# The low parts of two Down weights in each middle quarter: made by an accumulating transfer instead of VectorE, and used last in what is begun

## The chip, the cores and the metric

The kernel runs on one core of a Trainium2 chip. The core has a matrix engine (TensorE, PE in the profile; its weight loads are PEld), three engines for elementwise work (VectorE or DVE, ScalarE or ACT, GpSimd or POOL), and SyncE (SP), which here only issues transfers. Each engine works through its own list of instructions in order and waits at semaphores for the others. The metric is the device time of one execution in microseconds (us), the median of three runs.

## The reference

Two layers, each on 512 positions of width 1024: a gated feed-forward block (FFN) of inner width 2816, a mixer of three head groups, and a second FFN of the same form. The change lies in the FFNs, of which there are four in all:

```python
def swiglu(x, w1, w3, w2):
    return (jax.nn.silu(x @ w1) * (x @ w3)) @ w2
...
h = x + 0.5 * swiglu(rms_norm(x, ffn1_norm[l]), ffn1_w1[l], ffn1_w3[l], ffn1_w2[l])
```

The product with `w1` and `w3` is called Up here, that with `w2` Down. Everything is float32.

## The kernel before

**Precision by parts.** A float32 operand is kept as a high part, which the matrix engine takes at full speed, and a low part, which is the rest. A product is then three matmuls: high by high, high by low, low by high. `mm3` (lines 179 to 182) issues them. Its second line, 181, multiplies the weight's high part by the activation's low part, and line 182 the weight's low part (`wlo`) by the activation's high part (`ghi`). In the profile these three are the rows of L180, L181 and L182.

**Two ways to make the parts of a weight.** `weights` (line 164) loads a piece of weight from HBM into a tile `raw` and splits it. With V as its third argument, `split` (line 147) has ScalarE copy the high part (L148) and VectorE subtract it from `raw` (L149). With G, `split_by_dma` (line 151) has ScalarE write the high part (L153) and then its input with the sign turned (L154; the copy rounds as the high part does), and a transfer issued by GpSimd (L155) adds the weight from HBM a second time, so that the rest is left in the tile. The second way needs no VectorE, one more ScalarE operation, and one more transfer, which can start only when ScalarE is through.

**Stages of an FFN.** The 22 slices of 128 inner columns stand in four quarters of 6, 6, 6 and 4 (`QUARTERS`). For each quarter the Up products of its slices are made, two slices at a time. The first four slices are plain three-matmul products, the later ones (`up_pair`) go by a scheme with seven half-size products, which loads three more tiles of weights: `raw` and sums of weights, `wsum`, of which one half is again added by a transfer from GpSimd (L372). In the first three quarters the Up products of the next quarter's first pair come ahead of this quarter's Down products (`ahead`). Their matmuls are the rows of L383 and L391.

**Down.** For each of the eight blocks `d` of 128 output columns, `begin(d)` loads a weight of 128 x 768 numbers (384 KB), splits it (always with V before) and multiplies the first four of the quarter's six slices; then the last two follow, and VectorE adds the result to `h` (L611). That is 18 matmuls for each `d`, in one bank of PSUM. There are three banks of the kind `mm`, one of which the Up pair uses too, four pairs of tiles for weights' parts (`whi`, `wlo`), and three for `raw`.

**What sets the order.** The text of the program is not the order of issue. A planner puts each engine's instructions into a list when the kernel is built: it takes what is ready by its own reckoning of times, so that matmuls of a Down weight may stand between those of an Up pair. Some places have orders written by hand (`queued`, `issue_after`); `begin` in the first three quarters has none. The list is fixed at run time.

Of the kernel before, what the change touches and what calls it, by code (L numbers as in the profile page):

```python
# [16 lines left out]
ALL = slice(None)  # L17

P = 128
# [46 lines left out]
def trunk(ctx: ExitStack, tc: tile.TileContext, xT, memT, pos, w1a, w3a, w2a, w1b, w3b, w2b,  # L66
          wconv, wqk, wvm, wmem, wout, gains, small, rows, consts, out):
    nc = tc.nc
    V, G, A, T = nc.vector, nc.gpsimd, nc.scalar, nc.tensor
# [10 lines left out]
    turn, tail, hold, opening = [0], [None], {}, []  # L80
# [10 lines left out]
    def bank(shape, tag):  # L91

        if tag == "mm":
            return ps_mm.tile(shape, F32, tag=tag, name=tag)
        return ps_ax.tile(shape, F32, tag=tag, name=tag, bufs=1 if tag == "cf" else 2)
# [7 lines left out]
    def raw_tile(src, cols):  # L103
        raw = wst.tile([P, UNIT], F32, tag="raw", name="raw", bufs=3)
        raw_tile.at = nc.sync.dma_start(raw[:, 0:cols], src)
        return raw
# [40 lines left out]
    def split(hi, lo, x, on):  # L147
        a = A.activation(hi, x, AF.Copy)  # L148
        return a, on.tensor_tensor(out=lo, in0=x, in1=hi.bitcast(F32), op=ALU.subtract)  # L149

    def split_by_dma(hi, lo, x, src):

        A.activation(hi, x, AF.Copy)  # L153
        A.activation(lo, x, AF.Copy, scale=-1.0)  # L154
        G.dma_start(lo, src, accum_op=ALU.add)  # L155
# [6 lines left out]
    def pair():  # L162
        return (wst.tile([P, UNIT], F32R, tag="whi", name="whi"), wst.tile([P, UNIT], F32R, tag="wlo", name="wlo"))

    def weights(src, cols, on, own=None):
        hi, lo = own or pair()
        if first:
            raw = first.pop(0)
            for c in halves:
                opening.append(split(hi[:, c], lo[:, c], raw[:, c], V)[0])  # L170
            return hi, lo
        raw = raw_tile(src, cols)
        if on is G:
            split_by_dma(hi[:, 0:cols], lo[:, 0:cols], raw[:, 0:cols], src)
        else:
            weights.at = split(hi[:, 0:cols], lo[:, 0:cols], raw[:, 0:cols], on)[1]
        return hi, lo

    def mm3(ps, a, b, first, last, **more):
        T.matmul(ps, a[0], b[0], start=first, stop=False, **more)  # L180
        T.matmul(ps, a[0], b[1], start=False, stop=False, **more)  # L181
        tail[0] = T.matmul(ps, a[1], b[0], start=False, stop=last, **more)  # L182

    def at(p, *idx):
        return tuple(x[idx] for x in p)

    def blk(k, n=P):
        return slice(k * n, (k + 1) * n)
# [323 lines left out]
    def ffn(l, w13, w2, x, sums, factors, last, at_product, aside=None, closing=None):  # L512

        def up(f, i, among=(), spread_at=None):
            ps = bank([P, S], "po" if 2 * f + i in (3, 4) else "mm")
            with ExitStack() as held:
                for o in hold.get(2 * f + i, ()):
                    held.enter_context(tc.issue_after(o.ins))  # L520
                w = weights(w13[i][l, f], 1024, V if f == 0 or f < 3 and l == 0 and w13[0] is w1a else G)
            if not among:
                project(ps, w, x)
                return ps
            for k in range(KD):
                with queued():
                    project(ps, w, x, [k])
                for go in among[2 * k : 2 * k + 2]:
                    go()
                if k == spread_at:  # L530
                    r = sums()
                    with queued():
                        scale.append(factors(r))
            return ps

        def gate(pp, R, u, g, hi, lo):
            V.tensor_tensor(out=u, in0=pp[0], in1=R, op=ALU.mult)
            A.activation(u, u, AF.Silu)
            V.tensor_tensor(out=g, in0=pp[1], in1=R, op=ALU.mult)
            V.tensor_tensor(out=g, in0=g, in1=u, op=ALU.mult)  # L540
            split(hi, lo, g, V)

        g, products = {}, []
        for f in range(0, PLAIN, 2):
            g[f], g[f + 1] = gated()
        if first:

            w = [weights(None, 1024, V) for _ in range(2)]
            products = [bank([P, S], "mm") for _ in range(2)]
            steps = [(i, k, *z) for i in range(2) for k, *z in ((0, 0, 0), (0, 0, 1), (1, 0, 0), (1, 0, 1), (0, 1, 0), (1, 1, 0))]  # L550
            steps += [(i, k, *z) for k in range(2, KD) for i, *z in ((0, 0, 0), (0, 1, 0), (1, 0, 0), (1, 1, 0), (0, 0, 1), (1, 0, 1))]
            for n, (i, k, a, b) in enumerate(steps):
                with queued():
                    tail[0] = T.matmul(products[i], w[i][a][:, blk(k)], x[b][:, k, :], start=n in (0, 6), stop=n > 45)
            for d in range(KD):
                with tc.issue_after(opening[-1].ins):
                    squares.add(h[:, d, :])
        while len(products) < at_product:
            products.append(up(len(products) // 2, len(products) % 2))
        among, sums = sums()  # L560
        scale, own = [], w13[0] is w1a
        products.append(up(at_product // 2, at_product % 2, among, (6 if l else 4) if own else KD - 1))
        gain, R, after = scale[0]
        hold.update({i: [kept.at] for i in ((6,) if l else (4, 5))} if own else {})
        if own and not l:
            hold[3] = [squares.at, squares.sum_at]
        while own and not l and len(products) < 5:
            with queued():
                products.append(up(len(products) // 2, len(products) % 2))
        behind = raw_tile.at if own and not l else None  # L570
        M = Seven(normed(gain, R, weights.at if own and not l else None))
        with queued():
            for f in range(0, PLAIN, 2):
                u, v = (tmp.tile([P, 2, S], F32, tag=t, name=t, bufs=n) for t, n in (("u", 1), ("g", 2)))
                for j in range(2):
                    while len(products) < 2 * (f + j) + 2:
                        products.append(up(len(products) // 2, len(products) % 2))
                    gate(products[2 * (f + j) :], R, u[:, j], v[:, j], *g[f + j])
                if not f:
                    M.first()  # L580
        M.rest()
        hold.clear()
        for q, (f0, nf) in enumerate(QUARTERS):
            ahead = 2 if q + 1 < len(QUARTERS) else 0
            for f in range(f0, f0 + nf + ahead, 2):
                if f not in g:
                    g[f], g[f + 1] = up_pair(l, w13, f, M, f > QUARTERS[1][0], behind if f < QUARTERS[1][0] else None)
                    if f == PLAIN:
                        with tc.issue_after(M.gated.ins):
                            rescale = after()  # L590
            begun = []

            def begin(d):

                w = weights(w2[l, d, :, f0 * P : (f0 + nf) * P], nf * P, V)
                ps = bank([P, S], "mm")
                for j in range(nf - 2):
                    mm3(ps, at(w, ALL, blk(j)), g[f0 + j], j == 0, False)
                begun.append((ps, w))

            for d in range(KD if ahead or not closing else KD - 2):
                while len(begun) < (d + 1 if ahead or d else 3):
                    with nullcontext() if ahead or d else queued():
                        begin(len(begun))
                ps, w = begun[d]
                for j in range(nf - 2, nf):
                    mm3(ps, at(w, ALL, blk(j)), g[f0 + j], False, j == nf - 1)
                if not q and rescale:
                    with tc.issue_after((added if d else M.gated).ins):
                        rescale(d)  # L610
                added = V.scalar_tensor_tensor(out=h[:, d, :], in0=ps, scalar=0.5, in1=h[:, d, :], op0=ALU.mult, op1=ALU.add)  # L611
                if not ahead:
                    last(d)
                if aside and q == 2:
                    aside(d, added)
            if closing and not ahead:
                closing(l, f0, nf, g, [at(p, ALL, slice(0, nf * P)) for p in
                                       (weights(w2[l, d, :, f0 * P : (f0 + nf) * P], nf * P, V) for d in range(KD - 2, KD))])
# [765 lines left out]
```

## Time and profile before

| | us |
|---|---|
| median of three runs | 1751.15 (1750.63 to 1751.29) |
| the profiled execution, its own time | 1751.12 |
| its span, first to last instruction | 1749.3 |
| between span and time | 1.8 |

The profile is one execution. Its page gives the busy time of each engine; other views give waits (which instruction stood idle, and what ended that), a timeline (start, length, engine, line, operation, what it writes and reads, how many in a row), groups of like instructions, and transfers. A matmul's length in a row runs on into the next matmul's, since they are pipelined: for the pace of TensorE take the distance between starts.

### The profile page before, as it was taken

What the parts mean: (1) busy time and instruction counts of PE and PEld (TensorE: products, weight loads), DVE (VectorE), ACT (ScalarE), POOL (GpSimd) and SP (SyncE); (2) the same over time, 40 slices, a digit from 0 to 9 for tenths busy, and PEclk for the clock granted to TensorE, in tenths of its full rate; (3) what the DMA queues carried; (4) which work ended last, traced back from release to release, by engine and by line L of the source; (5) the groups of instructions that cost most, each with busy time, mean ns of one, the idle gap of its engine ahead of it and who ended that gap; (6) DMA issues with size and microseconds to landing.
All of it is one profiled execution on the core that took longest, in us unless ns stands there. A gap on an engine that the chain in (4) does not pass through costs nothing.

```text
span 1749.3 us, 25622 instructions
## 1 busy us (share of the span) xinstructions
PE 1735.9 (99%) x9556; PEld 1499.7 (86%) x9556; DVE 1398.0 (80%) x2330; ACT 904.4 (52%) x1437; POOL 193.9 (11%) x220
## 2 busy tenths in 40 slices
PE   9999999999999999999999999999999999999998
PEld 7988888888888988888889888888888889888886
DVE  7968789889877869686778796968898768696966
ACT  6635354555765535353655353535567655353533
POOL 1000000006121000000010000000251310000000
PEclk9999999999999999999999999999999999999999
DMA  8456565357247546464566474643671666474622
GB/s 276 128 140 178 135 166 147 103 160 169 82 93 184 137 131 175 136 177 137 154 146 169 123 185 118 176 140 106 169 161 49 145 145 181 124 186 127 171 79 85
DMA packets 96332, 253.43 MB, mean 145 GB/s; under 512 B 9808, under 2 KB 16208, under 8 KB 96208
## 3 DMA queue, kind: packets, MB, share of 16 engines
q1 hardware_dynamic: 77200, 190.45, 34.1%
q0 software_dynamic: 19008, 61.35, 20.1%
q8 instruction: 75, 1.23, 0.3%
q14 instruction: 49, 0.40, 0.1%
HBM read 249.67 MB, written 2.10 MB: 144 GB/s over the span
## 4 chain that ended last, share of the span: by engine, by line
PE 96%; DVE 2%; ACT 1%; DMA 1%; issue 0%; SPq 0%; DVEq 0%; ACTq 0%
PE po L391 15%; PE mm L180 14%; PE mm L182 14%; PE mm L181 14%; PE pt L391 9%; PE pt L383 8%; PE mm L391 2%; PE cf L391 2%; PE po L383 2%; PE po L180 2%; PE po L182 2%; PE po L181 2%; PE po L989 2%; PE mm L937 1%; PE cf L180 1%; PE cf L182 1%
## 5 line engine op out<-in xcount | busy, mean ns | idle before, releaser
L148 ACT ACTIVATE whi<-raw 128x1024 fp32r<-128x1024 f32 (+3 forms) x346 | 326.1, 948 | 434.0 <-PE mm L181 204.0
L149 DVE TENSOR_TENSOR wlo<-raw,whi 128x1024 fp32r<-128x1024 f32 (+3 forms) x346 | 374.3, 1090 | 70.9 <-ACT whi L148 51.6
L180 PE MATMUL mm<-ghi,whi 128*128 128x512 f32 (+1 forms) x752 | 292.1, 390 | 0.7 <-ACT ghi L508 0.4
L181 PE MATMUL mm<-glo,whi 128*128 128x512 f32 (+1 forms) x752 | 292.3, 389 | 0.0
L182 PE MATMUL mm<-ghi,wlo 128*128 128x512 f32 (+1 forms) x734 | 285.2, 389 | 0.0
L611 DVE SCALAR_TENSOR_TENSOR h<-mm,h 128x512 f32<-128x512 f32 x126 | 86.6, 690 | 139.4 <-PE mm L182 139.1
L180 PEld LDWEIGHTS mm<-ghi,whi 128*128 128x128 f32 x752 | 141.1, 188 | 30.6 <-ACT ghi L508 1.3
L181 PEld LDWEIGHTS mm<-glo,whi 128*128 128x128 f32 x752 | 141.2, 188 | 28.0 <-DVE glo L509 0.4
L182 PEld LDWEIGHTS mm<-ghi,wlo 128*128 128x128 f32 x734 | 137.8, 188 | 27.9
L391 PE MATMUL po<-xlo,whi 128*128 128x512 f32 x512 | 139.5, 394 | 0.0
L1119 DVE SCALAR_TENSOR_TENSOR there<-ypad,par,there 128x512 f32<-128x512 f32 x180 | 136.2, 781 | 1.3
L180 PE MATMUL mm<-xhi,whi 128*128 128x512 f32 x256 | 101.8, 398 | 0.0
L391 PEld LDWEIGHTS po<-xlo,whi 128*128 128x128 f32 x512 | 89.4, 188 | 13.3
L181 PE MATMUL mm<-xlo,whi 128*128 128x512 f32 x256 | 99.6, 389 | 0.0
L182 PE MATMUL mm<-xhi,wlo 128*128 128x512 f32 x256 | 99.5, 390 | 0.0
L148 ACT ACTIVATE whi<-wsum 128x1024 fp32r<-128x1024 f32 x72 | 75.7, 1051 | 33.8 <-PE mm L181 30.2
L149 DVE TENSOR_TENSOR wlo<-wsum,whi 128x1024 fp32r<-128x1024 f32 x72 | 87.8, 1219 | 2.7 <-ACT whi L148 2.7
L391 PEld LDWEIGHTS po<-xlo,wlo 128*128 128x128 f32 x512 | 78.2, 188 | 10.8
L391 PE MATMUL po<-xlo,wlo 128*128 128x256 f32 x512 | 81.3, 280 | 0.0
L440 ACT ACTIVATE part<-pt 128x256 f32<-128x256 f32 x112 | 42.0, 375 | 61.0 <-PE pt L391 61.0
L383 PE MATMUL pt<-mh,whi 128*128 128x256 f32 x512 | 71.7, 283 | 0.0
L383 PEld LDWEIGHTS pt<-mh,whi 128*128 128x128 f32 x512 | 66.6, 191 | 1.0
(410 smaller groups left out, 3659.8 us busy)
## 6 DMA issues: line engine op xcount, KB each, us to landing
raw<-in_w2a SPq DMA_DIRECT2D x48, 384.0 KB, 3.7
raw<-in_w2b SPq DMA_DIRECT2D x48, 384.0 KB, 3.8
raw<-in_w1a SPq DMA_DIRECT2D x26, 512.0 KB, 3.5
raw<-in_w3a SPq DMA_DIRECT2D x26, 512.0 KB, 3.7
raw<-in_w1b SPq DMA_DIRECT2D x26, 512.0 KB, 3.5
raw<-in_w3b SPq DMA_DIRECT2D x26, 512.0 KB, 4.0
wsum<-in_w1a SPq DMA_DIRECT2D x18, 512.0 KB, 6.6
wsum<-in_w3a SPq DMA_DIRECT2D x18, 512.0 KB, 3.8
```

The source lines that it names most:

```text
L148: a = A.activation(hi, x, AF.Copy)
L149: return a, on.tensor_tensor(out=lo, in0=x, in1=hi.bitcast(F32), op=ALU.subtract)
L180: T.matmul(ps, a[0], b[0], start=first, stop=False, **more)
L181: T.matmul(ps, a[0], b[1], start=False, stop=False, **more)
L182: tail[0] = T.matmul(ps, a[1], b[0], start=False, stop=last, **more)
L383: tail[0] = T.matmul(ps, w[part][:, blk(4 * half + q[0])], M.m[j][q[0]][:, q[1]], skip_group_check=True, start=first and not n, stop=n == 11)
L391: tail[0] = T.matmul(out, w[part][:, blk(4 * half + k)], M.m[j][k][:, 0:n], skip_group_check=True, start=first and not part and k == 0, st ...
L440: A.activation(part[i][:, t], x[i][:, 0], AF.Copy)
L611: added = V.scalar_tensor_tensor(out=h[:, d, :], in0=ps, scalar=0.5, in1=h[:, d, :], op0=ALU.mult, op1=ALU.add)
L937: tail[0] = T.matmul(pp[i][:, z, :], q, k, start=not masked, stop=True, skip_group_check=True)
L989: tail[0] = T.matmul(po[:, 2 * c + i, :], ptb[:, i, j, :], v, start=(j == 0), stop=(j == nk - 1))
L1119: V.scalar_tensor_tensor(out=cv[:, c, :], in0=ypad[:, c, j : j + S], scalar=conv_w[:, c, j : j + 1], in1=cv[:, c, :], op0=ALU.mult, op1=AL ...
```

## The change

`begin` takes a new branch for the first two blocks (`d < 2`) of the second and third quarters (`q` is not 0 and `ahead` is not 0), in each of the four FFNs: 2 x 2 x 4 = 16 of the 128 Down weights. There `weights` is called with G, so the low part is made by ScalarE and an accumulating transfer. And the order in which the four slices' matmuls stand in the program is another one: first the high part of the weight by both parts of the activations for all four slices (8 matmuls), then the low part of the weight for all four (4 matmuls). The last two slices are multiplied by `mm3` as before. The number of matmuls is the same.

```diff
             def begin(d):
 
-                w = weights(w2[l, d, :, f0 * P : (f0 + nf) * P], nf * P, V)
+                late = d < 2 and q and ahead
+                w = weights(w2[l, d, :, f0 * P : (f0 + nf) * P], nf * P, G if late else V)
                 ps = bank([P, S], "mm")
                 for j in range(nf - 2):
-                    mm3(ps, at(w, ALL, blk(j)), g[f0 + j], j == 0, False)
+                    if not late:
+                        mm3(ps, at(w, ALL, blk(j)), g[f0 + j], j == 0, False)
+                        continue
+                    for i in range(2):
+                        T.matmul(ps, w[0][:, blk(j)], g[f0 + j][i], start=j == i == 0, stop=False)
+                for j in range(nf - 2 if late else 0):
+                    tail[0] = T.matmul(ps, w[1][:, blk(j)], g[f0 + j][0], start=False, stop=False)
                 begun.append((ps, w))
```

## The prediction

> **What bounds the kernel now.** I read the page first: the busy time of each engine, then the share of each engine in the chain that ended last, then the two kinds of transfer.
>
> ```profile
> span 1749.3 us, 25622 instructions
> PE 1735.9 (99%) x9556; PEld 1499.7 (86%) x9556; DVE 1398.0 (80%) x2330; ACT 904.4 (52%) x1437; POOL 193.9 (11%) x220
> ...
> q1 hardware_dynamic: 77200, 190.45, 34.1%
> q0 software_dynamic: 19008, 61.35, 20.1%
> ...
> PE 96%; DVE 2%; ACT 1%; DMA 1%; issue 0%; SPq 0%; DVEq 0%; ACTq 0%
> ```
>
> TensorE is busy 1735.9 of 1749.3 us and makes 96% of the last chain; VectorE, which the change relieves, makes 2%. But a busy PE could still be waiting inside its pipeline, so next comes the view of waits for PE alone (who waited on whom: us in total, times, longest). It has 11 rows; the first, the two of Down's first matmul, and the last are:
>
> ```profile
> PE mm L554 <- ACT whi L148: 1.2, 1, 1.2
> ...
> PE mm L180 <- ACT ghi L508: 0.4, 2, 0.2
> ...
> PE mm L180 <- ACT whi L148: 0.3, 1, 0.3
> ...
> PE pt L383 <- ACT xlo L148: 0.2, 1, 0.2
> ```
>
> Eleven waits, none over 1.2 us, and no row in which PE waits for VectorE's `wlo` (L149). For Down there is one of 0.3 us. So I look for what the change could break rather than for what it could free, and take one of its eight places apart: the second quarter of the second FFN. The timeline of PE there:
>
> ```profile
> 701.42 0.40 PE L180 MATMUL mm<-ghi,whi 128*128 128x512 f32 x1
> 701.65 0.40 PE L181 MATMUL mm<-glo,whi 128*128 128x512 f32 x1
> 701.88 1.09 PE L391 MATMUL po<-xlo,whi 128*128 128x512 f32 x4
> ...
> 703.27 0.40 PE L180 MATMUL mm<-ghi,whi 128*128 128x512 f32 x1
> ...
> 707.14 0.39 PE L182 MATMUL mm<-ghi,wlo 128*128 128x512 f32 x1
> 707.36 1.07 PE L391 MATMUL pt<-xhi,whi 128*128 128x512 f32 x4
> ...
> 708.74 0.40 PE L182 MATMUL mm<-ghi,wlo 128*128 128x512 f32 x1
> 708.98 1.09 PE L391 MATMUL po<-xlo,whi 128*128 128x512 f32 x4
> ...
> 711.78 0.40 PE L180 MATMUL mm<-ghi,whi 128*128 128x512 f32 x1
> ```
>
> One weight is begun with two matmuls at 701.42, the other does all its 18 from 703.27 to 707.36, and the first goes on at 708.74 and 711.78. Between them stand the last 32 matmuls of the Up pair: 8 at 701.88, 8 at 707.36, 16 at 708.98. From 703.27 to 707.14 there are 17 steps in 3.87 us, 0.228 us each: no gap. Here are the two weights' parts on ScalarE and VectorE, and VectorE's last read of a bank that the 16 matmuls need:
>
> ```profile
> 699.32 0.85 ACT L148 ACTIVATE whi<-raw 128x768 fp32r<-128x768 f32 x1 [1.42 <-issue]
> 700.07 0.36 ACT L440 ACTIVATE part<-pt 128x256 f32<-128x256 f32 x1
> 701.14 0.85 ACT L148 ACTIVATE whi<-raw 128x768 fp32r<-128x768 f32 x1 [0.71 <-PE po L391]
> ...
> 701.37 0.95 DVE L149 TENSOR_TENSOR wlo<-raw,whi 128x768 fp32r<-128x768 f32 x1
> 702.24 0.42 DVE L402 TENSOR_TENSOR part<-part,pt 128x256 f32<-128x256 f32 x1
> 702.57 0.95 DVE L149 TENSOR_TENSOR wlo<-raw,whi 128x768 fp32r<-128x768 f32 x1
> ...
> 704.10 0.42 DVE L402 TENSOR_TENSOR g<-g,po 128x256 f32<-128x256 f32 x1
> ```
>
> I read the other seven places too: the same order, but for one, shown below, that runs 0.5 us behind.
>
> **The change part by part.** Groups of instructions (count, busy us, mean ns), one GpSimd issue, and two rows of transfers (KB each, median us from issue to landing), then the landing of all of L155's:
>
> ```profile
> L149 DVE TENSOR_TENSOR wlo<-raw,whi 128x768 fp32r<-128x768 f32 x96 | 91.6, 955 | 19.1 <-ACT whi L148 18.0
> L154 ACT ACTIVATE glo<-raw 128x768 fp32r<-128x768 f32 x8 | 6.7, 842 | 0.3 <-PE pt L724 0.2
> ...
> 704.83 0.86 POOL L372 DMA_DIRECT2D wsum<-in_w1b  x1 [7.58 <-DVE g L402]
> ...
> glo<-in_wvm POOLq DMA_DIRECT2D x8, 384.0 KB, 8.8
> ...
> DMA to landing us min/median/max: 5.8/8.2/11.8
> ```
>
> Removed: 16 subtractions of 0.955 us, 15.3 us of VectorE. PE does not wait for them anywhere, so they are worth nothing by themselves: 0. What stands behind them on VectorE (the additions of L402) comes up to 1.9 us earlier in each place; that only lets the 24 Up matmuls left after 703.27 go sooner, which is not less work.
>
> Added on ScalarE: 16 copies of 0.842 us, 13.5 us. The second weight's high part, now written from 701.14 to 701.99, comes at most 0.84 us later, 702.83, still ahead of 703.27: 0, with 0.44 us of cover. If that cover is gone, it costs 0.4 us a place at most. `raw` is free after ScalarE's second copy rather than VectorE's subtraction, at 701.3 instead of 702.32, so the next loads from SP start no later.
>
> Added on POOL: 16 issues of 0.86 us, on an engine busy 11%. Ahead of or behind the second one stands L372's issue at 704.83, which waits for its own data; see the rivals.
>
> Added on the DMA engines: 16 transfers of 0.393 MB (384 KB). Queue 0 holds the accumulating ones: 20.1% of 1749.3 us for 61.35 MB is 5.73 us of all sixteen engines per MB, so 2.25 us each, 4.5 a place. That is not free just there. Busy time of the stretches (us, PE, PEld, DVE, ACT, POOL, clock, DMA share, GB/s):
>
> ```profile
> 701.80:707.80 6.00, 6.00 (x30) 5.01 (x29) 3.62 (x9) 1.89 (x5) 0.86 (x1) 1.00 0.97 309
> 707.80:713.80 6.00, 6.00 (x33) 5.15 (x32) 5.86 (x12) 2.92 (x5) 0.00 (x0) 1.00 0.77 194
> 713.80:719.80 6.00, 6.00 (x28) 4.94 (x28) 4.44 (x7) 2.36 (x4) 0.00 (x0) 1.00 0.48 140
> ```
>
> Free are 0.2 us, then 1.4, then 3.1: the backlog is gone by about 719.5 (estimate). It falls on the two low parts, on L372's sums, which are read in the next quarter, or on the Down weights behind, which PE reaches after 712.
>
> Moved: the low part's 4 matmuls go behind 8 others. The wait this brings is the only term that can count. The first low part: high part ready at 700.17, L440 to 700.43, second copy to about 701.3, issue 701.3, landing 8.8 us later (the median for the same size) 710.1; by the ends of L155's row 707.1 to 713.1. The second: 702.8 and 8.8 is 711.6, by the ends 708.6 to 714.6. What PE has without any low part, from 701.42: 2 matmuls (to 701.88), 8 of the Up pair (to 703.27), 8 high ones of the second weight (1.82, to 705.09), 8 of Up (708.74 - 707.36 = 1.38, to 706.47), 16 of Up (711.78 - 708.98 = 2.80, to 709.27; their banks are free at 704.52), 6 high ones of the first weight (1.37, to 710.64). There it needs a low part. If it is the first weight's: there since 710.1, no wait; 4 low matmuls and the last six (2.28) lead to 712.9, and the second's is there since 711.6. No wait again. If it is the second weight's, 711.6 - 710.6 = 1.0 us. A third weight could fill 18 x 0.228 = 4.1 us more, once its bank is free.
>
> The Trainium skill ("DMA: Bandwidth & Descriptors", on the anatomy of one DMA, the GpSimd path) fits 2.0 us and bytes / 436e3 to a transfer from GpSimd. That would be 2.9 us (an estimate by the page): low parts at 704.2 and 705.7, no wait in any order, the same time, and next to no chance for the first rival below. The trace speaks against it, with 5.8 us as the shortest of L155; I go by the row.
>
> Sum: 0 removed, 0 added on engines, wait 0 in eight places: the profiled execution's 1751.12, of which 1749.3 is its span and 1.8 lies around it; the median is 1751.15. I predict **1751.2**.
>
> **The rivals.** *Slower: the low part's matmuls stand in PE's list ahead of its landing.* The list is fixed, so PE then waits with work behind it. Place: the first `wlo` matmul in the eight stages. If the second weight's low part is taken first, 1.0 us x 8 = 8: 1759. If the planner reckons with the shortest landing (708.6 for the second) and the chip needs the median (711.6), 3.0 x 8 = 24: 1775. It decides from 0.44 us a place, 3.5 us in all. For it: the DMA engines at 97% just there. Against it: no row of PE's waits names a transfer, though L155 and L372 are used all through the kernel.
>
> *Slower: the transfers get in each other's way.* It has happened once, in the second quarter of the first FFN:
>
> ```profile
> 175.69 0.86 POOL L372 DMA_DIRECT2D wsum<-in_w3a  x1 [8.79 <-DMA wsum<-in_w3a]
> 176.25 0.33 SPq L105 DMA_DIRECT2D raw<-in_w2a  x1
> ...
> 182.75 0.85 ACT L148 ACTIVATE whi<-raw 128x768 fp32r<-128x768 f32 x1 [2.41 <-DMA raw<-in_w2a]
> ...
> 183.65 0.50 PE L180 MATMUL mm<-ghi,whi 128*128 128x512 f32 x1 [0.31 <-ACT whi L148]
> ```
>
> A load issued behind an accumulating transfer came 6.5 us later, and PE stood 0.31 us. Eight times that is 2.5 us, 1753.6, still within 0.2%. It is more if the second accumulating transfer stands behind L372 on POOL: issue 704.83 + 0.86 = 705.7, landing 714.5 against 712.9, 1.6 us; in the four second quarters, where the timeline has this L372, 6.4 us: 1757.5.
>
> *Faster.* PE's whole waiting in Down is 0.7 us (0.4 and 0.3 above): 1750.4 if all of it went. A better pace from the new order could add to it; but the step is 0.228 from L180 to L181, with the same part of the weight, and from L181 to L182, with another. 0.2% would take 3.5 us, and no row offers that.
>
> *It doesn't do what it says*: the low part made on GpSimd's path but used at once, because the planner mixes the groups. That is the first rival's second price.
>
> **How the numbers follow.** 0.2% (3.5 us) is about what a measurement of this kernel can tell from no change. No wait that counts: 0.56. Low part ahead of its landing: 0.32. Transfers in each other's way by more than 3.5 us: 0.08. Faster: 0.04. So faster 0.04, same 0.56, slower 0.40. The range begins at 1750.3, the faster case, and goes to 1768, a wait of 2.1 us in each place, between the first rival's prices; some 0.15 lie above and 0.03 below. By itself the likeliest case has 1750.6 to 1754.
>
> **What would show it.** VectorE: 80 instead of 96 subtractions of 128x768 on `raw`, about 15 us less busy. ScalarE: 16 rows of L153 and L154 with 128x768 from Down weights. POOL: 16 more issues of L155; queue 0 at 67.6 MB. PE: 9556 matmuls. Right: no row "PE mm <- DMA wlo" of more than a few tenths, and L391's `po` and `pt` matmuls moved ahead of the low parts. Wrong: such a row eight times, with 1 to 3 us each, or PE waiting for `whi` behind late loads. An increase of the time without any new wait of PE would break the whole argument.

## The result, and the profile after

| | before | after |
|---|---|---|
| median, us | 1751.22 (4 runs, 1750.63 to 1751.84) | 1762.28 (4 runs, 1761.94 to 1763.12) |
| ratio, with its 95% interval | | 1.0064 [1.0051, 1.0077] |
| span of the profiled execution, us | 1749.3 | 1760.2 |

The change makes the kernel 11.1 us slower. That lies inside the predicted range (1750.3 to 1768), but the case called likeliest, no wait that counts, did not happen, and the forecast itself, 1751.2, is 11 us too low.

The lines of the page of after that answer to those shown of before: the span, the busy time of each engine, the two kinds of transfer (packets, MB, share of sixteen engines), and the shares of the chain that ended last.

```profile
span 1760.2 us, 25659 instructions
PE 1740.2 (99%) x9556; PEld 1501.4 (85%) x9556; DVE 1384.4 (79%) x2314; ACT 916.1 (52%) x1453; POOL 208.8 (12%) x236
...
q0 software_dynamic: 21312, 67.64, 21.4%
...
PE 90%; DMA 5%; DVE 3%; ACT 1%; issue 1%; POOL 0%; SPq 0%; DVEq 0%; POOLq 0%; ACTq 0%
```

The change did what it says: VectorE has 16 operations fewer and is 13.6 us less busy, ScalarE has 16 more (11.7 us), POOL 16 more, and queue 0 moved 6.29 MB more. PE makes the same 9556 matmuls, but its share of the last chain fell from 96% to 90%, and transfers went from 1% to 5%. Which transfers, the view of PE's waits of after says (us in total, times, longest):

```profile
PE mm L605 <- DMA wlo<-in_w2b: 5.1, 4, 2.1
PE mm L605 <- DMA wlo<-in_w2a: 2.4, 3, 1.4
```

L605 is the new line with the low part's four matmuls. Seven waits, 7.5 us, where before no row named a transfer. That is close to the mark by which the prediction said it would be wrong (such a row eight times, 1 to 3 us each): the seven are 0.4 to 2.1 us long and stand in five of the eight stages. The second quarter of the second FFN, which the prediction took apart, is the worst. Its stage starts at 690.33 us (first Down load issued); here are GpSimd's issues there and ScalarE's copies of the sign-turned high part, from the timeline of after:

```profile
700.85 0.84 ACT L154 ACTIVATE wlo<-raw 128x768 fp32r<-128x768 f32 x1
...
702.68 0.83 ACT L154 ACTIVATE wlo<-raw 128x768 fp32r<-128x768 f32 x1
...
701.98 0.86 POOL L155 DMA_DIRECT2D wlo<-in_w2b  x1 [4.32 <-DVE part L402]
705.92 0.86 POOL L372 DMA_DIRECT2D wsum<-in_w1b  x1 [3.08 <-DMA wsum<-in_w1b]
706.46 1.22 POOL L155 DMA_DIRECT2D wlo<-in_w2b  x1
```

The second low part's transfer could have been issued when ScalarE was through, at 703.5. It was issued at 706.46, behind L372 in POOL's list. L372 adds the second half to a sum of weights (`wsum`) for the next Up pair, and it stood 3.08 us for the load of that sum's first half (L371). That is what the stages have in common: that load lands 13.98 to 15.04 us into the stage, and L372 is issued 0.55 us behind it, in each of the five stages that have such a sum there. In the other three stages POOL's list has no sum between the two low parts.

PE in the same place (timeline of after):

```profile
709.32 0.63 PE L391 MATMUL po<-xlo,wlo 128*128 128x256 f32 x4
710.50 0.50 PE L605 MATMUL mm<-ghi,wlo 128*128 128x512 f32 x1 [0.54 <-DMA wlo<-in_w2b]
...
712.22 0.86 PE L605 MATMUL mm<-ghi,wlo 128*128 128x512 f32 x3
...
714.06 0.39 PE L182 MATMUL mm<-ghi,wlo 128*128 128x512 f32 x1
716.54 1.72 PE L605 MATMUL mm<-ghi,wlo 128*128 128x512 f32 x4 [2.10 <-DMA wlo<-in_w2b]
718.07 0.63 PE L180 MATMUL mm<-ghi,whi 128*128 128x512 f32 x1
718.49 0.63 PE L181 MATMUL mm<-glo,whi 128*128 128x512 f32 x1
...
720.53 0.40 PE L180 MATMUL mm<-ghi,whi 128*128 128x512 f32 x1
```

After 714.06 PE has nothing in its list but the second block's low part, and stands until that lands. Behind the stop its steps are 0.43 us (718.07 to 718.49) instead of 0.23.

Worked out from the timelines of all eight stages, in us from each stage's first Down load (the second low part's issue, its landing, and the start of its four matmuls, which is 23.16 where nothing waits):

| stage | sum between | issued | landed | matmuls |
|---|---|---|---|---|
| 1st FFN, 2nd quarter | yes | 15.36 | 23.94 | 23.98 |
| 2nd FFN, 2nd quarter | yes | 16.13 | 26.17 | 26.21 |
| 2nd FFN, 3rd quarter | yes | 15.62 | 24.77 | 24.82 |
| 3rd FFN, 2nd quarter | yes | 15.93 | 25.31 | 25.36 |
| 4th FFN, 2nd quarter | yes | 15.07 | 24.28 | 24.33 |
| 1st, 3rd, 4th FFN, 3rd quarter | no | 13.47, 14.77, 13.47 | 21.13, 20.99, 20.74 | 23.16 |

The delays of the five add up to 0.82 + 3.05 + 1.66 + 2.20 + 1.17 = 8.9 us (1.25 of it from first low parts that landed late, 0.7 in the second and 0.55 in the third FFN). The slow steps behind the longest stop cost 1.7 us more (716.54 to 720.53 are ten steps, 3.99 us instead of 2.28). Together 10.6, where the spans differ by 10.9.

### The profile page after: what moved, and what is told of

The parts are those of the page before. It is cut to its first block, busy times and chain, and to the rows that moved or that the text cites. A ratio compares the mean times of both kernels' runs of the same rounds, so it can differ in the third digit from the quotient of the medians.

```text
span 1760.2 us, 25659 instructions
## 1 busy us (share of the span) xinstructions
PE 1740.2 (99%) x9556; PEld 1501.4 (85%) x9556; DVE 1384.4 (79%) x2314; ACT 916.1 (52%) x1453; POOL 208.8 (12%) x236
## 4 chain that ended last, share of the span: by engine, by line
PE 90%; DMA 5%; DVE 3%; ACT 1%; issue 1%; POOL 0%; SPq 0%; DVEq 0%; POOLq 0%; ACTq 0%
PE mm L180 13%; PE mm L181 13%; PE mm L182 13%; PE po L391 13%; PE pt L383 8%; PE pt L391 8%; PE cf L391 2%; PE po L383 2%; PE mm L391 2%; PE po L180 2%; DMA wlo<-in_w2b 2%; PE po L182 2%; PE po L181 2%; PE po L996 2%; PE mm L944 1%; DMA wsum<-in_w1a 1%
## 5 line engine op out<-in xcount | busy, mean ns | idle before, releaser
L148 ACT ACTIVATE whi<-raw 128x1024 fp32r<-128x1024 f32 (+3 forms) x330 | 312.6, 952 | 436.0 <-PE mm L181 192.3
L149 DVE TENSOR_TENSOR wlo<-raw,whi 128x1024 fp32r<-128x1024 f32 (+3 forms) x330 | 358.8, 1095 | 87.4 <-ACT whi L148 68.8
L180 PE MATMUL mm<-ghi,whi 128*128 128x512 f32 (+1 forms) x688 | 267.5, 391 | 0.4 <-ACT ghi L508 0.4
L181 PE MATMUL mm<-glo,whi 128*128 128x512 f32 (+1 forms) x688 | 267.7, 389 | 0.0
L182 PE MATMUL mm<-ghi,wlo 128*128 128x512 f32 x670 | 260.5, 389 | 0.0
L180 PEld LDWEIGHTS mm<-ghi,whi 128*128 128x128 f32 x688 | 129.5, 188 | 28.6 <-ACT ghi L508 1.3
L181 PEld LDWEIGHTS mm<-glo,whi 128*128 128x128 f32 x688 | 129.5, 188 | 26.4 <-DVE glo L509 0.4
L182 PEld LDWEIGHTS mm<-ghi,wlo 128*128 128x128 f32 x670 | 126.1, 188 | 25.8
L149 DVE TENSOR_TENSOR wlo<-wsum,whi 128x1024 fp32r<-128x1024 f32 x72 | 87.7, 1217 | 2.7 <-ACT whi L148 2.7
```

## The experiments

Three theories stood after the result. **A**: the second low part's issue stands on POOL behind the waiting L372, and PE's fixed list comes to its matmuls before it lands. **B**: sixteen more transfers in a stretch where the DMA engines are full make every landing late, whatever the order of issue. **C**: the new order of matmuls costs by itself, in pace or in banks. Edits are shown against the changed kernel, with what is left out marked by three dots; "before" is always the kernel before, timed beside it.

**The low parts ahead of the sums on POOL.** The sums' accumulating transfers are held until both low parts' transfers have been issued. PE's list in the eight stages is the same. The edit holds more than the one sum between: each second quarter (and the third quarter of the second FFN) has three sums behind the low parts now, the other third quarters two, and of these the changed kernel issued one 3 to 8 us before the stage and one about 6 us into it, ahead of both low parts.

```diff
-        G.dma_start(lo, src, accum_op=ALU.add)
+        split_by_dma.at = G.dma_start(lo, src, accum_op=ALU.add)
...
-            G.dma_start(x, w13[i][l, f + 1], accum_op=ALU.add)
+            with tc.issue_after(down_low[0].ins) if down_low else nullcontext():
+                G.dma_start(x, w13[i][l, f + 1], accum_op=ALU.add)
...
                 w = weights(w2[l, d, :, f0 * P : (f0 + nf) * P], nf * P, G if late else V)
+                if late:
+                    down_low[:] = [split_by_dma.at]
```

> The changed kernel with one edge more: on POOL the accumulating transfer for the next pair's sum (L372 in the changed kernel) is issued behind both low parts. PE's list stays as in the changed kernel. Theory A (the second low part stands in POOL's queue behind a sum whose own load is late): the second low part is issued about 13.5 us after the stage's first Down load instead of 15.1 to 16.1, lands at about 21 as in the three stages without such a sum, and the waits at the low matmuls fall from about 11 us in all to under 1: 1751 to 1752.5. Theory B (the sixteen DMA engines are full there, whatever POOL's order): landing stays at 24 or later and over half of the waits stay: 1757 or more. Theory C (the new order of the matmuls costs by itself): 1760 to 1763.

Measured: 1753.27 us against 1750.82, ratio 1.0012 [1.0003, 1.0022]. Nine of the 11 us are gone; it is 0.8 us above what A gave. In the third FFN's second quarter (stage start 1038.04), GpSimd's timeline of this kernel, whose lines stand one or two lower (L156 is after's L155, L374 its L372):

```profile
1049.69 0.86 POOL L156 DMA_DIRECT2D wlo<-in_w2a  x1 [23.55 <-ACT wlo L155]
1051.51 0.86 POOL L156 DMA_DIRECT2D wlo<-in_w2a  x1 [0.96 <-ACT wlo L155]
1052.05 1.22 POOL L374 DMA_DIRECT2D wsum<-in_w1a  x1
1052.58 1.58 POOL L374 DMA_DIRECT2D wsum<-in_w3a  x1
1053.12 1.93 POOL L374 DMA_DIRECT2D wsum<-in_w1a  x1
```

The second low part is issued 13.5 us into the stage in all eight places, and lands at 20.8 to 22.6; no matmul of the second block waits for it. In the five stages this landing is earlier by more than the issue: the transfer itself took 7.8 to 9.1 us instead of 8.6 to 10.0, and since two more sums were moved behind it, this run alone doesn't part A from B. But the issue is enough by itself: 13.47 and the lengths that the five had in after make landings of 22.1 to 23.5, against a need at 23.16, or 23.9 in the stage that has the 23.5. So A holds for most of the time. What is left at the low parts is the waits on the *first* one, which lands 5.9 to 8.3 us after its issue; they delay three stages of the profiled execution by 2.1 us in all. Of the 1.35 in the worst of them 0.7 is a later issue (12.34 instead of 11.65, behind ScalarE); the rest is the transfer's length, which is B's cause. That execution, the slowest of the ten, is 3.6 us longer than before's; 1.1 of the rest is a wait at 333.37, outside the stages that the change touches (`PE po L393 <- DVE u L404`). The view of PE's waits has the first low part as

```profile
PE mm L609 <- DMA wlo<-in_w2b: 1.3, 2, 1.1
```

**The order alone.** The new order of matmuls, with the low parts from VectorE again.

```diff
-                w = weights(w2[l, d, :, f0 * P : (f0 + nf) * P], nf * P, G if late else V)
+                w = weights(w2[l, d, :, f0 * P : (f0 + nf) * P], nf * P, V)
```

> The new order of the matmuls, but the low parts from VectorE as before, so no added transfer and nothing added on ScalarE. A and B: no wait at the low matmuls, 1750.7 to 1751.5, as before the change. C: most of the 11 us is there, 1757 or more.

Measured: 1751.59 against 1750.82, ratio 1.0003 [0.9994, 1.0013], span 1749.4, and no wait for `wlo` among PE's. That is 0.1 above what was expected. C falls: the order costs nothing that can be measured.

**The transfer alone.** The low parts by transfer, with the matmuls in the old order.

```diff
-                late = d < 2 and q and ahead
-                w = weights(w2[l, d, :, f0 * P : (f0 + nf) * P], nf * P, G if late else V)
+                slow = d < 2 and q and ahead
+                late = False
+                w = weights(w2[l, d, :, f0 * P : (f0 + nf) * P], nf * P, G if slow else V)
```

> The low parts by the accumulating transfer, but the matmuls in the old order (three for each slice). In PE's list the first low matmul then stands 6.5 us behind the first matmul of the stage (2 + 8 Up + 2 + 8 Up + 16 Up), that is at about 18.1 us, where the first low part lands at 17.7 to 20.1. A and B: waits of about 1 us at the first low part in each of eight stages and 1 to 3 us at the second in five: 1764 to 1770. C: below the changed kernel's time, 1751 to 1757.

Measured: 1779.16 against 1750.82, ratio 1.0158 [1.0143, 1.0174], more than was expected. PE's waits in this kernel:

```profile
PE mm L182 <- DMA wlo<-in_w2b: 10.3, 6, 2.4
PE mm L182 <- DMA wlo<-in_w2a: 8.2, 5, 2.5
```

18.5 us in 11 waits. Behind four of them the granted clock fell (see the last section); counted from windows of 1 us, each fall cost 1.6 to 1.7 us, 6.7 in all. Together that is 25 of the 28 us by which the span is longer than before's; no row names the other 3. So the two halves of the change aren't alike: given the transfer, the new order saves 17 us, and without the transfer (the run above) the order wins nothing.

**Other work in front of the second block's low part.** The third block is begun before the second block's four low matmuls, which now follow the third's 12: 12 x 0.228 = 2.7 us of cover. POOL's list is as in after.

```diff
-                for j in range(nf - 2 if late else 0):
-                    tail[0] = T.matmul(ps, w[1][:, blk(j)], g[f0 + j][0], start=False, stop=False)
                 begun.append((ps, w))
+                if not late:
+                    return
+
+                def low():
+                    with queued() if d else nullcontext():
+                        for j in range(nf - 2):
+                            tail[0] = T.matmul(ps, w[1][:, blk(j)], g[f0 + j][0], start=False, stop=False)
+                lows[d] = low
...
-                while len(begun) < (d + 1 if ahead or d else 3):
+                while len(begun) < (d + 1 + (d == 1 and q > 0) if ahead or d else 3):
...
+                if d in lows:
+                    lows[d]()
```

> The changed kernel, but the second block's four low matmuls stand in PE's list behind the 12 matmuls with which the third block begins (2.7 us), so the second low part is needed at about 26 instead of 23 us. POOL's order is that of the changed kernel. A and B alike (a fixed list with the low part ahead of its landing): only the first low part's waits of about 1 us in all and some tenths at the second stay, 1751.5 to 1753.5. If the time goes into anything but that wait (pace, bandwidth): over 1757.

Measured: 1753.06, ratio 1.0014 [1.0005, 1.0024]. In the stages with a sum between the second low part is still issued at 15.2 to 16.2 and lands at 24.3 to 25.7, as in after; but its matmuls stand at 25.88 (26.4 to 26.6 where the first low part was late), and no block waits for it. The landing is as late as before and costs nothing: what counted is where the list has its reader. What is left is again the first low part (three waits, 1.0 us, in the profiled execution).

**Only the first block by transfer.**

```diff
-                late = d < 2 and q and ahead
+                late = d < 1 and q and ahead
```

> The change for block 0 alone, not block 1: one low part a stage by transfer, issued on POOL ahead of the sum. A: its landing at 18 to 20 us is ahead of its use at about 20.8, no waits: 1750.8 to 1751.8. B: half of the load, half of the loss: 1755 to 1757.

Measured: 1752.16 against 1750.79, ratio 1.0007 [0.9999, 1.0016]; no wait of PE for `wlo`. The first low part is issued 11.7 us into the stage (12.3 in one), ahead of the sum, and lands by 19.9; in this kernel's list its four matmuls stand at 20.87. The median is 0.4 us above what A gave and far below B. What the profiled execution lost, it lost elsewhere: its span is 2.4 us longer than before's, and 1.6 of that come from waits at 331 to 334 us, outside the stages that the change touches.

**Only the second block by transfer.** The same line with `d == 1`.

> The change for block 1 alone: as many transfers as with block 0 alone, but in POOL's queue this one stands behind the sum in five of eight stages. It is needed at about 23.1 us. A: issued at 15 to 16 and landing at 22.5 to 24.5, it is late by up to 1.4 us in those five stages and not in the other three: 1751.5 to 1756, slower than with block 0 alone. B: the same time as with block 0 alone.

Measured: 1754.22, ratio 1.0022 [1.0014, 1.0031]. GpSimd's timeline and PE's, in the third FFN's second quarter of this kernel (stage start 1035.68):

```profile
1050.50 0.86 POOL L372 DMA_DIRECT2D wsum<-in_w1a  x1 [7.76 <-DVE g L402]
1051.03 1.22 POOL L155 DMA_DIRECT2D wlo<-in_w2a  x1
```

```profile
1058.56 0.40 PE L182 MATMUL mm<-ghi,wlo 128*128 128x512 f32 x1
1059.41 1.19 PE L605 MATMUL mm<-ghi,wlo 128*128 128x512 f32 x4 [0.45 <-DMA wlo<-in_w2a]
```

The same standing behind L372, in the same five stages, issued at 15.3 to 15.9. But with one low part in the stage instead of two it lands 6.9 to 8.3 us after its issue (after: 8.6 to 10.0), between 22.7 and 23.7, and is needed at 23.1. So in after the late issue makes 1.6 to 2.7 us of the later landing, and the company of the first low part's transfer another 1.0 to 2.8 (one trace of each): A's place, and some of B in its price. The single transfer lands on the edge: the profiled execution has only this one wait at a low part, and its span, 1751.1, is 1.3 us short of what the median stands for (1754.2 less 1.8 around the span), and the eleven runs go from 1752.85 to 1759.33. Which of the five stages loses more in the other executions no trace here shows.

**Only the third quarters.** The condition is `d < 2 and q == 2`: four stages, of which one has the sum between.

> The change in the third quarters alone (four stages of eight). Only in one of these four does a sum stand between the two low parts on POOL. A: the loss is that one stage's, about 1.8 us: 1752.5 to 1753.5. B: half of the loss, 1756 to 1757.5.

Measured: 1755.46, ratio 1.0026 [1.0015, 1.0037]; 2 us above what A alone gave. The profiled execution's span is 1753.7, and its waits

```profile
PE mm L605 <- DMA wlo<-in_w2b: 2.0, 3, 1.4
...
PE po L391 <- DVE u L402: 0.7, 1, 0.7
```

The 1.4 is the second low part in the one stage with a sum, so that stage pays as in after. Worked out from the timeline, it lost 2.2 us, and another stage lost 0.5 at a first low part: 2.7 of the 4.4 us by which the span is longer than before's. The second row stands at 332.75, outside the changed stages, and the kernel with the order alone, which has no added transfer, has it too (0.3 us, at 332.06); about 0.6 us were lost by there. The rest, about 1 us, stays open. A by itself is too low here, and the measured time is nearer to B's 1756.

**Both remedies.** The low parts ahead of the sums on POOL, and the third block in front of the second's low part.

> Both cures: low parts ahead of the sums on POOL, and the second low part's matmuls behind the third block's beginning. A: no wait at a low part at all, 1750.5 to 1751.5, the same as before the change within 0.1%; nothing in the profile says it could be faster by more than the 0.3 us that PE waited for a high part in one stage. B: 1753 or more.

Measured: 1751.37 against 1750.79, ratio 1.0002 [0.9993, 1.0011], span 1749.8; one wait for `wlo` is left, 0.7 us. That is the kernel before again, and not better: 14 us less work on VectorE bought nothing where PE is busy 99% of the time. No kernel here beats the one before.

## Why the prediction was right in its range and wrong in its mechanism

That 1762.28 lies inside the range is in part luck. The range reaches up to 1768 for a wait of 2.1 us in each of eight places; what came was five places with 0.8 to 3.1 us and a fall of the clock that no case had. The likeliest case, no wait that counts, did not come.

**Right: what the removed work was worth.** The 16 subtractions were costed at 0, since no row of PE's waits named L149. With every cost of the transfers taken out again (both remedies), the time is that of before within its interval. ScalarE's 16 copies at 0, too: none of PE's new waits names it.

**Nearly right: when PE needs the low parts.** The prediction counted PE's list to 710.64 and 712.9, that is 20.8 and 23.1 us into the stage. In after they stand at 19.46 (where nothing waits) and 23.16; the first is 1.4 us earlier than thought, because one low matmul stands ahead of the last eight of the Up pair. And the first weight's low part does come first.

**Wrong: "The second: 702.8 and 8.8 is 711.6".** This is the step that failed. It starts the transfer when ScalarE is through, and costs POOL's 16 issues at nothing because the engine is busy 11%. The prediction had L372's issue at 704.83 before it, and left open on which side the transfer would stand. It stands behind. Issued 16.1 us into the stage instead of 13.0, it landed at 26.2 instead of 21.8, and the sum's "wait 0 in eight places" became 0.8 to 3.1 us in five. Put the low parts ahead of L372, and nine of the eleven us are gone.

The row that would have settled it was in the trace of before: L372 there is issued 14.4 to 15.0 us into the stage in five places, each 0.55 us after its load's landing, and ScalarE's finish at 13.0 is before that. What remained was the order of POOL's list, which the planner sets by its own reckoning; with both orders possible and one of them priced at 1.6 us a place, that order deserved a better chance than a share of the 0.08 for transfers in each other's way.

**The rivals.** "It is more if the second accumulating transfer stands behind L372 on POOL" was the mechanism, with a landing of 24.7 us into the stage; the five measured 23.9 to 26.2, 24.9 on average. Its price, 1757.5, was too low for three reasons: five stages have such a sum, not four (the third quarter of the second FFN was overlooked); first low parts land late in two, 1.25 us; and the clock's 1.7 us were not foreseen. The first rival, the low part's matmuls in PE's list ahead of the landing, names the same wait from PE's side, with prices of 1759 and 1775; the time came between them, at 1.4 us for each of eight places or 2.2 for each of the five. The two were one chain with two links, queue and list, and each remedy broke one link.

**Too narrow: the transfer's length.** 8.8 us is the median of the one row of the same size (`glo<-in_wvm`), over transfers elsewhere in the kernel; here the second of two in one stage, behind the sum's, took 8.6 to 10.0, one alone behind it 6.9 to 8.3. In the stage taken apart that is 1.2 us of the 4.4 by which the landing was later than forecast; the issue makes the other 3.1. The prediction's table of DMA shares (0.97 of the engines' time in the six us after 701.8) said that they would be in each other's way, and its term for this was 0. In after the stretch looks like this (us, PE, PEld, DVE, ACT, POOL, clock, DMA share, GB/s):

```profile
700.00:706.00 6.00, 6.00 (x34) 5.18 (x34) 3.92 (x11) 4.53 (x8) 0.94 (x2) 1.00 0.98 256
706.00:712.00 6.00, 5.46 (x30) 4.51 (x29) 3.16 (x8) 1.12 (x3) 1.68 (x2) 1.00 1.06 261
```

and the same stretches of before, 0.52 us earlier:

```profile
699.48:705.48 6.00, 6.00 (x34) 5.20 (x34) 5.70 (x13) 2.72 (x6) 0.65 (x1) 1.00 1.00 301
705.48:711.48 6.00, 6.00 (x33) 5.10 (x32) 3.78 (x7) 2.33 (x4) 0.21 (x1) 1.00 0.87 187
```

The first stretch was full already; the second, in which both low parts are under way, went from 0.87 to full. A landing there isn't the median's. (One small reading: the eleven rows of PE's waits before are thirteen waits, as two rows stand for two each. Nothing hangs on it.)

## What to carry to other kernels

Before giving an engine's queue a new transfer, read what stands ahead of it in that queue and what *that* waits for; a queue that is 11% busy can hold an issue for 3 us behind one waiting instruction. In a kernel where one engine is busy 99%, taking work from an engine that it never waits for was worth nothing here, while each new dependence could cost, so the change has to show which wait it ends. Where an operand's arrival is uncertain by some us, the fixed list should have as much other work ahead of its reader (here 12 matmuls made a landing of 25.7 us harmless), or the issue should be moved up.

## What the runs showed of the hardware

**TensorE's clock fell behind some stops of 1.8 to 2.5 us.** Windows of after around the longest stop (columns as above; the clock is the seventh):

```profile
714.30:716.60 2.30, 0.20 (x2) 0.06 (x1) 2.11 (x3) 0.84 (x1) 0.00 (x0) 1.00 0.79 255
716.60:720.30 3.70, 3.70 (x10) 2.86 (x11) 0.58 (x1) 0.00 (x0) 0.00 (x0) 0.55 0.38 115
```

and of the kernel with the transfer alone, around a stop of 2.38 us and around one of 1.96:

```profile
715.70:718.70 3.00, 3.00 (x7) 2.38 (x8) 2.90 (x5) 0.58 (x1) 0.00 (x0) 0.50 1.05 224
...
811.70:815.00 3.30, 3.30 (x14) 2.74 (x15) 1.81 (x3) 0.00 (x0) 0.00 (x0) 1.00 1.04 253
```

Some 3 to 3.7 us at about half the clock behind the first two, none behind the third; in after that cost 1.7 us on top of a wait of 2.1. The Trainium skill ("TensorE: Matmul & The Clock Gate", Part 1: The HAM clock gate) puts half the clock after an idle window of about 3.4 us. These stops are shorter, so here the measurement decides. All 11 stops of the kernel with the transfer alone tell more. The three longest (2.32, 2.38 and 2.46 us) were followed by the fall at once. Of two stops of 1.83 us, each with 3.9 us of matmuls and another stop (1.29 and 1.58 us) ahead of it, the one that ended at 195.37 was followed by it 1.3 us later (windows around it, below), the one that ended at 1603.50 was not; and neither was the 1.96. So below 2 us the length alone does not decide it; what else does, these runs don't show.

```profile
193.50:195.40 1.90, 0.07 (x2) 0.03 (x1) 1.82 (x3) 1.78 (x3) 0.00 (x0) 1.00 1.02 334
195.40:196.60 1.20, 1.20 (x5) 1.01 (x6) 1.04 (x2) 0.00 (x0) 0.00 (x0) 1.00 0.45 79
196.70:199.70 3.00, 3.00 (x9) 2.35 (x8) 0.00 (x0) 0.00 (x0) 0.00 (x0) 0.52 0.30 111
```

**A waiting issue holds the next one.** The Trainium skill ("DMA: Bandwidth & Descriptors", Anatomy of one DMA) says that a transfer's wait for a semaphore happens on the issuing sequencer, before dispatch. The trace agrees: L372 stood 3.08 us, and L155, whose data had been ready for 3.0 us, was issued right behind it, 16.1 us into the stage; put ahead of the sum it went at 13.5.
